# Adding an accumulator's two halves on ScalarE and GpSimd instead of TensorE

## The chip, the cores and the metric

One core of a Trainium2 chip runs the kernel. The metric is the device time of one execution in microseconds (us). The engines are TensorE (PE in the profile, its weight loads PEld), VectorE (DVE), ScalarE (ACT), GpSimd (POOL) and SyncE (SP), which here only starts DMA transfers. Each engine works through its own queue of instructions in the order in which the program wrote them, and a wait holds everything behind it on that engine.

## The reference

One layer of an encoder step for 288 tokens of width 2048: attention, a cross attention, a first norm, and then a mixture of 16384 single-neuron experts (128 x 128 product keys), of which each token chooses 128. The part that matters here is the experts' first product and its activation:

```python
def block(args):
    xs, es, gs = args
    act = jnp.einsum('td,tkd->tk', xs, u_tab[es], preferred_element_type=jnp.float32)
    h = (jax.nn.gelu(act, approximate=False) * gs).astype(xs.dtype)
    return jnp.einsum('tk,tkd->td', h, v_tab[es])
```

## The kernel before

The kernel treats 224 tokens densely: for them it computes the activations of all 16384 experts, in 128 blocks of 128 experts, sets the gates of the experts that were not chosen to zero, and multiplies with the value table. For the other 64 tokens it gathers the rows of the chosen experts with indirect DMAs on GpSimd (`fetch`, L944) and VectorE multiplies them (`use_u`, L963, into the gathered rows `ur`).

TensorE works on `float32r` operands of limited precision, so every large tensor is split into two parts: `hi` is a cast on ScalarE (L165), `lo` the remainder, raw minus hi, on VectorE (L181). The weights arrive as a stream of 128x1024 pieces, two per expert block ("half blocks"), through four raw buffers and three buffers each of `hi` and `lo`. `take` hands out the next piece and issues the cast of the piece two further on.

For one expert block (loop at L1031) an accumulator bank `ps` of 448 columns is filled by 16 pairs of products. The first of a pair multiplies `hi` with both parts of the tokens, `ux[:, d]`, side by side (448 columns, L1039). The second adds `lo` times the whole part (224 columns, L1041). So the left half of the bank holds the larger products and those of `lo`, and the right half the smaller ones, and both halves have to be added. `finish_act` (L989) does it, as a generator: it advances by one step at each `tick`, and there is a tick in the middle and at the end of every half block. Its first step comes right behind the block's last product: ScalarE copies the right half into `small`. At the next tick a product of `small` with the identity matrix adds it to the left half in the bank (L994). At the tick behind that ScalarE applies the Gelu from the bank into the block's row of the activations in SBUF, `hrow(i)` in the tensor `bigA` (L997).

`tick` also lets "slow" jobs proceed (mostly the choice of the experts, on VectorE, by a table of costs and a rate per tick), and then issues the `lo` that are due. From block 64 (`G0`) on the gates are built from one-hot matrices; until then `gated` is 0. The order of all engines' work is the order of this program text; nothing is rearranged later.

Of the kernel before, what the change touches and what calls it, by code (L numbers as in the profile page):

```python
# [9 lines left out]
F32 = mybir.dt.float32  # L10
# [4 lines left out]
OP = mybir.AluOpType  # L15
AX = mybir.AxisListType

P = 128
# [31 lines left out]
def tile_stream_step(ctx: ExitStack, tc, xT_d, xn_d, memT_d, ckT_d, cv_d, cmkT_d, cmv_d,  # L50
# [22 lines left out]
    def split_to(hi, lo, raw):  # L73
        """raw = hi + lo exactly, each part in the 12 bits that one pass of the tensor engine carries"""
        nc.scalar.copy(hi, raw)
        nc.vector.tensor_sub(lo, raw, hi.bitcast(F32))

    # x1 rows of the gathered tokens, and the expert choices
    keep = ctx.enter_context(tc.tile_pool(name="keep", bufs=1))
# [24 lines left out]

    # ------------------------------------------------ the stream of everything large
    def flat(t, a, b):
# [42 lines left out]
    def stream(n, ahead=AHEAD):  # L149
        """splits up to the weights that are ahead units after unit n, and loads beyond them"""  # L150
        until = n
        while until + 1 < len(plan) and ahead:
            until += 1
            ahead -= plan[until][2] is None
        while at["split"] <= until:
            k = at["split"]
            while at["load"] <= k:
                load_next()
            src, cols, hi, lo = plan[k]
            raw = loaded.pop(k)[:, :cols]  # L160
            if hi is None:
                hi, lo = own.get(k) or (strm.tile([P, 1024], F32R, tag=t, name=f"{t}{k}")[:, :cols] for t in ("hi", "lo"))
                parts[k] = (hi, lo)
            for cs in pieces(k):
                nc.scalar.copy(hi[:, cs], raw[:, cs])  # L165
                pending.append((k, hi[:, cs], lo[:, cs], raw[:, cs]))
                if k in PIECES:
                    settle()
            at["split"] += 1
        while at["load"] <= min(until + RAW - AHEAD, len(plan) - 1):  # L170
            load_next()
# [5 lines left out]
    def settle():  # L177
        """the small parts that are due"""
        while pending:
            _, hi, lo, raw = pending.pop(0)  # L180
            nc.vector.tensor_sub(lo, raw, hi.bitcast(F32))  # L181
# [23 lines left out]

    # ------------------------------------------------ work beside the stream
    stages = []          # each advances by one stage per tick
    slow = deque()       # one at a time, by its cost on the vector engine
    pace = {"rate": 0.0, "left": 0.0}
# [19 lines left out]
    def mm_tile(ps, part, k, d, mh, ml, n):  # L229
        """out^T [128 columns, n tokens] += one contraction tile of weights' (mh + ml)"""  # L230
        wh, wl = (w[:, k * P:(k + 1) * P] for w in part)
        nc.tensor.matmul(ps[:, :n], wh, mh[:, d, :n], start=(d == 0), stop=False)  # L232
        nc.tensor.matmul(ps[:, :n], wh, ml[:, d, :n], start=False, stop=False)  # L233
        nc.tensor.matmul(ps[:, :n], wl, mh[:, d, :n], start=False, stop=(d == DT - 1))  # L234

    def mm_unit(ps, half, mh, ml, n, ticks=(3, 7), tiles=8):
        """the next unit's contraction tiles"""
        part = take()
        for k in range(tiles):
            mm_tile(ps, part, k, half * 8 + k, mh, ml, n)  # L240
            for _ in range(ticks.count(k)):
                tick()

    def keep_warm(n):
        """products into a bank that nobody reads, so that the tensor engine's clock stays up over a pause"""
        ps = pb()
        for _ in range(n):
            nc.tensor.matmul(ps[:, :P], ident, ident, start=True, stop=True)
# [7 lines left out]
    def rsqrt(pool, out, v, n, rows=P):  # L256
        """out = (v + eps) ** -0.5, with a Newton step behind the square root's table"""
        t = pool.tile([P, 3, n], F32, tag=f"rs{n}", name=f"rs{num()}")[:rows]
# [7 lines left out]

    # ------------------------------------------------ constants, memory projections
    stream(-1, 1)
# [23 lines left out]
    def bias_job():  # L292
        """the relative bias of all heads, laid out by diagonals through DRAM"""
        for h in range(HEADS):
            ps = pb()
            nc.tensor.matmul(ps[:, :NREL], relb[:, h], hot, start=True, stop=True)
            yield
            nc.scalar.copy(bvec[:, h], ps[:, :NREL])
        nc.gpsimd.dma_start(bias_s, bvec.rearrange("p a b -> p (a b)"))
# [28 lines left out]

    # ------------------------------------------------ mixers
    ats = ExitStack()  # L330
# [44 lines left out]
    def diff_attend(h, qT, kT, vT, ck, cv):  # L375
# [51 lines left out]
        def weights(t):  # L427
            # w * s0 = e0 - lam * s0 / s1 * e1
            rows = TT[t][1]
# [153 lines left out]

    # ------------------------------------------------ output projection, first norm
    x1s = ExitStack()
# [26 lines left out]
    def residual(c, ps):  # L612
        """the tokens' rows again, added to the residual"""
        ot = nwk.tile([P, 3, P], F32, tag="ot", name=f"ot{c}", bufs=5)
# [46 lines left out]

    # ------------------------------------------------ expert choice
    ROWS = (P, 96, P)

    def topk(units):
        """the 16 best experts of heads for the tokens of their tiles: scores, and both halves of their numbers;
        the units' steps take turns"""
        V = nc.vector
# [88 lines left out]
    def dense_choice(t):  # L757
        """the choices of a dense token tile, its heads' units done"""
        yield from gates(t, 8)
# [25 lines left out]
    def rows_job():  # L785
        """x1 rows of the gathered tokens"""
        for a in range(2):
# [7 lines left out]
    def copy_job():  # L795
        """the dense tokens' part of x1, both parts side by side"""
        for d4 in range(4):
# [12 lines left out]
    def normed_turn(c):  # L810
        """a tile of the normed rows, transposed"""
        tp = pb()
# [100 lines left out]
    for q in range(2, 16):  # L913
        done(q, proj(x1h, x1l, NTOK))
    # the last scores, before the units of the experts
    while stages:
# [6 lines left out]

    # ------------------------------------------------ experts: activations and gates
    gat = ctx.enter_context(tc.tile_pool(name="gat", bufs=3))
# [5 lines left out]
    def hrow(i):  # L931
        return bigA[:, i] if i < SPLIT else big[1][2][:, i - SPLIT]
# [4 lines left out]
    class Rows:  # L937
        """half rows of the gathered tokens' experts, fetched ahead of their use"""

# [26 lines left out]
    def one_hots(t0):  # L966
        """of two tokens: the second key's choices, and the gates at the first key's"""
        Bt = big[2].tile([P, 2, NKEY], F32, tag="ohB", name=f"ohB{t0}")
# [9 lines left out]
    def gate_in(t0, ps, done):  # L978
        """gates of four tokens for all experts: into h where the activation is there, aside elsewhere"""
        pg = ps.rearrange("p (t i) -> p i t", t=4)  # L980
# [8 lines left out]
    def finish_act(i, ps, gated):  # L989
        """the smaller products onto the others, and the activation; h where the gates are there"""  # L990
        small = tmpp.tile([P, ND], F32R, tag="small", name=f"small{i}")
# [85 lines left out]

    # ------------------------------------------------ experts: values
    vw = ctx.enter_context(tc.tile_pool(name="vw", bufs=2, side="right"))
# [33 lines left out]
    def evac(half, dt, acc):  # L1113
        """the smaller products onto the others, and the sum onto the residual"""
        d = half * 8 + dt
# [21 lines left out]
    def finish_gathered():  # L1137
        """the gathered tokens' halves together, their second norm, out"""
        up = [gat.tile([P, 1024], F32, tag="rows", name=f"up{c}") for c in range(2)]
# [17 lines left out]
        for c in range(2):  # L1157
# [8 lines left out]
            if c == 0:  # L1166
# [3 lines left out]
                yield 4.0  # L1170
        # the rows of the dense tokens' norm, into what is free now
        for c in range(2):
# [12 lines left out]
    def turn(g, t):  # L1185
        """rows of a quarter of the columns again, in a free bank"""
        R = rows2[t]
# [8 lines left out]
    def products(half, dt, part, i):  # L1196
        """columns of the values (hi + lo) . a block's h, whole and remainder"""
        hb = batches[(half * NKEY + i) // 4][:, i % 4] if half or i else h0
# [7 lines left out]
    def finish(half, dt):  # L1206
        """a finished accumulator's evacuation, begun; the one before it, ended"""
        g = evac(half, dt, accs[dt])
# [65 lines left out]

    # ------------------------------------------------ second norm of the dense tokens
    fin = ctx.enter_context(tc.tile_pool(name="fin", bufs=1))
# [116 lines left out]
```

## Time and profile before

| | |
|---|---|
| runs | 2011.85, 2012.72, 2016.64 us; median 2012.72 |
| profiled execution | span 2008.1 us; a time of its own beside the span is not listed |
| busy in the whole span | PE 99%, PEld 93%, DVE 78%, ACT 58%, POOL 24% |
| expert blocks, first product | about 624 to 1336 us |
| of these the first 62 blocks | about 624 to 944 us |

The span goes from the first to the last instruction of one execution recorded by the profiler. Busy times of TensorE include the overlap of neighbouring products, so a single product's duration is longer than what it adds to the time. A name such as `lo<-raw,hi` is the tile that an instruction writes and those that it reads.

### The profile page before, as it was taken

To read this page: it belongs to the slowest core of one execution; us is meant where nothing else is said; L and a number is where in the kernel's file an instruction comes from. 1 tells how busy PE (TensorE), PEld (TensorE's weight loads), DVE (VectorE), ACT (ScalarE), POOL (GpSimd) and SP (SyncE) were. 2 spreads that over 40 slices of the span, in tenths; PEclk is the share of its full clock that TensorE was granted. 3 is DMA by queue.
4 is the path that set the end of the run, shared out by engine and by line. 5 is a ranking of instruction groups with operands and counts; after the bars stand their busy time and mean duration, and the time that the engine had idled before them with its cause. 6 is when DMAs were issued, how large, how long until landed. Compare 5 with 4: busy or idle time off the path is not lost.

```text
span 2008.1 us, 34989 instructions
## 1 busy us (share of the span) xinstructions
PE 1983.6 (99%) x13178; PEld 1872.5 (93%) x13178; DVE 1567.3 (78%) x2683; ACT 1160.7 (58%) x1919; POOL 480.9 (24%) x348
## 2 busy tenths in 40 slices
PE   9999999999999999999999999999999999999996
PEld 7999999999999999999999999999999999999996
DVE  5455555556788889998899999978888888888886
ACT  5345545544534555555999999854455555444553
POOL 0110000010000112222333333324443343334412
PEclk9999999999999999999999999999999999999998
DMA  8854555484445788888888888889999998999985
GB/s 294 258 165 141 153 155 153 129 287 137 154 148 162 241 291 280 277 282 283 294 298 296 293 298 302 300 288 318 335 322 343 327 333 314 323 328 321 327 264 167
DMA packets 147625, 521.21 MB, mean 260 GB/s; under 512 B 16848, under 2 KB 21088, under 8 KB 147328
## 3 DMA queue, kind: packets, MB, share of 16 engines
q1 hardware_dynamic: 103504, 360.49, 54.8%
q0 software_dynamic: 43952, 158.48, 22.0%
q8 instruction: 104, 1.70, 0.3%
q14 instruction: 65, 0.53, 0.1%
HBM read 508.33 MB, written 10.06 MB: 258 GB/s over the span
## 4 chain that ended last, share of the span: by engine, by line
PE 96%; DMA 1%; DVE 1%; ACT 1%; POOL 0%; issue 0%; SPq 0%; POOLq 0%; ACTq 0%; DVEq 0%
PE pa L1039 22%; PE pa L1200 11%; PE pb L1200 11%; PE pa L1041 11%; PE pa L232 8%; PE pa L233 7%; PE pa L234 7%; PE pb L1202 5%; PE pa L1202 5%; PE pb L1019 3%; DMA raw<-in_wmk 1%; PE pa L994 1%; PE pb L397 0%; DVE lo L181 0%; PE pa L893 0%; PE pa L319 0%
## 5 line engine op out<-in xcount | busy, mean ns | idle before, releaser
L181 DVE TENSOR_TENSOR lo<-raw,hi 128x1024 fp32r<-128x1024 f32 (+1 forms) x679 | 820.8, 1211 | 367.1 <-ACT hi L165 356.7
L165 ACT CAST hi<-raw 128x1024 fp32r<-128x1024 f32 (+1 forms) x679 | 705.5, 1040 | 497.2 <-PE pa L1200 253.8
L1039 PE MATMUL pa<-ux,hi 128*128 128x448 f32 x2048 | 669.8, 379 | 0.0
L1041 PE MATMUL pa<-ux,lo 128*128 128x224 f32 x2048 | 543.6, 265 | 0.0
L1039 PEld LDWEIGHTS pa<-ux,hi 128*128 128x128 f32 x2048 | 385.4, 188 | 29.4 <-issue 0.2
L1041 PEld LDWEIGHTS pa<-ux,lo 128*128 128x128 f32 x2048 | 391.7, 191 | 0.0
L948 POOL DMA_INDIRECT ur<-in_u,gidx x128 | 197.9, 1546 | 700.2 <-DVE ur L963 329.8
L1200 PE MATMUL pa<-hs,hi 128*128 128x448 f32 x1020 | 338.3, 376 | 0.0
L1200 PE MATMUL pb<-hs,hi 128*128 128x448 f32 x1020 | 338.0, 376 | 0.0
L948 POOL DMA_INDIRECT vr<-in_v,gidx x128 | 221.4, 1730 | 354.7 <-DVE x1g L1111 321.2
L1202 PE MATMUL pb<-hs,lo 128*128 128x224 f32 x1020 | 271.1, 266 | 0.3 <-DVE lo L181 0.3
L1202 PE MATMUL pa<-hs,lo 128*128 128x224 f32 x1020 | 271.0, 266 | 0.0
L1200 PEld LDWEIGHTS pb<-hs,hi 128*128 128x128 f32 x1020 | 191.4, 188 | 17.5
L1200 PEld LDWEIGHTS pa<-hs,hi 128*128 128x128 f32 x1020 | 191.4, 188 | 17.4
L1202 PEld LDWEIGHTS pb<-hs,lo 128*128 128x128 f32 x1020 | 195.1, 191 | 0.5 <-DVE lo L181 0.5
L232 PE MATMUL pa<-xh,hi 128*128 128x288 f32 x640 | 195.2, 305 | 0.0
L1202 PEld LDWEIGHTS pa<-hs,lo 128*128 128x128 f32 x1020 | 195.1, 191 | 0.0
L233 PE MATMUL pa<-xl,hi 128*128 128x288 f32 x640 | 188.9, 295 | 0.0
L234 PE MATMUL pa<-xh,lo 128*128 128x288 f32 x640 | 188.2, 294 | 0.0
L1111 DVE SCALAR_TENSOR_TENSOR x1g<-vr,ggate,x1g 128x1024 f32<-128x1024 f32 x128 | 163.7, 1279 | 0.0
L963 DVE SCALAR_TENSOR_TENSOR ur<-ur,x1g 128x1024 f32<-128x1024 f32 x128 | 155.7, 1216 | 0.0
L232 PEld LDWEIGHTS pa<-xh,hi 128*128 128x128 f32 x640 | 120.0, 188 | 4.9 <-issue 3.7
(346 smaller groups left out, 2706.7 us busy)
## 6 DMA issues: line engine op xcount, KB each, us to landing
raw<-in_ut SPq DMA_DIRECT2D x256, 512.0 KB, 4.4
raw<-in_v SPq DMA_DIRECT2D x255, 512.0 KB, 6.5
raw<-in_win SPq DMA_DIRECT2D x80, 512.0 KB, 3.7
raw<-in_wq SPq DMA_DIRECT2D x32, 512.0 KB, 3.6
raw<-in_wo SPq DMA_DIRECT2D x29, 512.0 KB, 3.7
raw<-in_wmv SPq DMA_DIRECT2D x8, 512.0 KB, 5.3
raw<-in_wmk SPq DMA_DIRECT2D x6, 512.0 KB, 5.8
xn<-in_xn POOLq DMA_DIRECT2D x8, 384.0 KB, 9.7
```

The costliest lines, as they stand in the source:

```text
L165: nc.scalar.copy(hi[:, cs], raw[:, cs])
L181: nc.vector.tensor_sub(lo, raw, hi.bitcast(F32))
L232: nc.tensor.matmul(ps[:, :n], wh, mh[:, d, :n], start=(d == 0), stop=False)
L233: nc.tensor.matmul(ps[:, :n], wh, ml[:, d, :n], start=False, stop=False)
L234: nc.tensor.matmul(ps[:, :n], wl, mh[:, d, :n], start=False, stop=(d == DT - 1))
L948: nc.gpsimd.indirect_dma_start(out=t, out_offset=None, in_=self.table, in_offset=bass.IndirectOffsetOnAxis(ap=gidx[:, a, s:s + 1], axis=0))
L963: nc.vector.scalar_tensor_tensor(rows, rows, 1.0, x1g[:, a * 1024:(a + 1) * 1024], op0=OP.mult, op1=OP.mult, accum_out=gact[:, a, s:s + 1])
L1039: nc.tensor.matmul(ps[:, :2 * ND], wh, ux[:, d].rearrange("p a t -> p (a t)"), start=(d == 0), stop=False, skip_group_check=True)
L1041: nc.tensor.matmul(ps[:, :ND], wl, ux[:, d, 0], start=False, stop=False, skip_group_check=True)
L1111: nc.vector.scalar_tensor_tensor(va, rows, ggate[:, s:s + 1], va, op0=OP.mult, op1=OP.add)
L1200: nc.tensor.matmul(accs[dt][:, :2 * ND], wh, hb.rearrange("p a t -> p (a t)"), start=(i == 0), stop=False, skip_group_check=True)
L1202: nc.tensor.matmul(accs[dt][:, :ND], wl, hb[:, 0], start=False, stop=False, skip_group_check=True)
```

## The change

For blocks 0 to 61 (`i < G0 - 2`) the accumulator's two halves are both copied to SBUF by ScalarE, the left half into the block's row of `bigA`, the right one into a tile `other`. At the next tick GpSimd adds the two, in place in `bigA`. Two ticks later ScalarE applies the Gelu, from `bigA` to `bigA`. Blocks 62 to 127 do as before. (Comments are dropped too, which moves line numbers: lines behind the new code are 10 higher.)

```diff
     def finish_act(i, ps, gated):
+        if i < G0 - 2:
+            other = tmpp.tile([P, ND], F32, tag="tmp", name=f"other{i}")
+            nc.scalar.copy(hrow(i), ps[:, :ND])
+            nc.scalar.copy(other, ps[:, ND:2 * ND])
+            yield
+            nc.gpsimd.tensor_tensor(out=hrow(i), in0=hrow(i), in1=other, op=OP.add)
+            yield
+            yield
+            nc.scalar.activation(hrow(i), hrow(i), AF.Gelu)
+            return
         small = tmpp.tile([P, ND], F32R, tag="small", name=f"small{i}")
         nc.scalar.copy(small, ps[:, ND:2 * ND])
         yield
         nc.tensor.matmul(ps[:, :ND], identr, small, start=False, stop=True, skip_group_check=True)
```

ScalarE's queue at the end of the first expert block, before (`hi` are the casts of the weights, `pa` the accumulator's bank):

```order
L165 CAST hi_6879<-raw_6767 128x1024
L992 CAST small_6901<-pa_6846 128x224
L165 CAST hi_6904<-raw_6850 128x1024
L997 ACT_TABLE_LOAD
L997 ACTIVATE bigA<-pa_6846 128x224
L165 CAST hi_6938<-raw_6882 128x1024
L992 CAST small_6960<-pa_6903 128x224
```

The same place in the changed kernel:

```order
L165 CAST hi_6879<-raw_6767 128x1024
L993 COPY bigA<-pa_6846 128x224
L994 COPY other_6901<-pa_6846 128x224
L165 CAST hi_6905<-raw_6850 128x1024
L165 CAST hi_6938<-raw_6882 128x1024
L999 ACT_TABLE_LOAD
L999 ACTIVATE bigA<-bigA 128x224
L993 COPY bigA<-pa_6904 128x224
```

There are two copies where there was one, and the Gelu stands behind the second cast instead of the first.

GpSimd's queue where the gathers of rows (`ur`) begin, before:

```order
L948 DMA ur_1_7617<-in_u,gidx 128x1024
L948 DMA ur_0_7701<-in_u,gidx 128x1024
L948 DMA ur_1_7763<-in_u,gidx 128x1024
L948 DMA ur_0_7852<-in_u,gidx 128x1024
L948 DMA ur_1_7930<-in_u,gidx 128x1024
```

And in the changed kernel:

```order
L948 DMA ur_1_7628<-in_u,gidx 128x1024
L996 TENSOR_TENSOR bigA<-bigA,other_7657 128x224
L948 DMA ur_0_7714<-in_u,gidx 128x1024
L996 TENSOR_TENSOR bigA<-bigA,other_7716 128x224
L948 DMA ur_1_7777<-in_u,gidx 128x1024
L996 TENSOR_TENSOR bigA<-bigA,other_7779 128x224
L996 TENSOR_TENSOR bigA<-bigA,other_7831 128x224
L948 DMA ur_0_7867<-in_u,gidx 128x1024
```

The adds are put between the gathers, one per expert block; TensorE's queue is 62 products shorter, and VectorE's is the same.

## Rows read from the trace of the kernel before

**Rows 1.** The page: busy us of the whole span, share, instructions.
```profile
PE 1983.6 (99%) x13178; PEld 1872.5 (93%) x13178; DVE 1567.3 (78%) x2683; ACT 1160.7 (58%) x1919; POOL 480.9 (24%) x348
```
**Rows 2.** Waits of TensorE, 624 to 965 us: total us, times, longest.
```profile
PE pb L832 <- ACT qT L860: 0.5, 1, 0.5
```
**Rows 3.** Busy us by stretch: PE, PEld, DVE, ACT, POOL; clock, DMA share, GB/s.
```profile
684.00:724.00 40.00, 40.00 (x259) 38.00 (x258) 37.90 (x98) 21.25 (x31) 12.10 (x8) 1.00 0.88 303
...
774.00:794.00 20.00, 20.00 (x130) 19.00 (x129) 19.27 (x45) 10.81 (x16) 4.29 (x3) 1.00 0.86 284
...
814.00:864.00 50.00, 50.00 (x322) 47.51 (x321) 47.27 (x115) 26.21 (x40) 12.68 (x8) 1.00 0.83 276
...
874.00:934.00 60.00, 60.00 (x385) 57.02 (x384) 55.81 (x124) 31.12 (x47) 11.38 (x9) 1.00 0.86 281
...
sum 340.00, PE 340.00 PEld 322.95 DVE 301.47 ACT 191.25 POOL 62.40; mean PE 37.78 PEld 35.88 DVE 33.50 ACT 21.25 POOL 6.93
```
**Rows 4.** Timeline of TensorE around one L994: start us, duration us.
```profile
801.44 0.27 PE L1041 MATMUL pa<-ux,lo 128*128 128x224 f32 x1
801.54 0.27 PE L994 MATMUL pa<-small,identr 128*128 128x224 f32 x1
801.65 0.37 PE L1039 MATMUL pa<-ux,hi 128*128 128x448 f32 x1
```
**Rows 5.** The same without L994, at the border of two half blocks.
```profile
722.48 0.26 PE L1041 MATMUL pa<-ux,lo 128*128 128x224 f32 x1
722.59 0.38 PE L1039 MATMUL pa<-ux,hi 128*128 128x448 f32 x1
722.80 0.27 PE L1041 MATMUL pa<-ux,lo 128*128 128x224 f32 x1
```
**Rows 6.** The chain of waits, 620 to 970 us, shares by line.
```profile
by line: PE pa L1039 64.6%; PE pa L1041 31.4%; PE pa L994 2.0%; PE pb L1019 0.5%; PE pa L232 0.4%; PE pa L234 0.3%; PE pa L233 0.3%; PE pb L763 0.2%; PE pb L832 0.1%; ACT qT L860 0.1%; PE pb L834 0.1%; PE pb L833 0.1%; issue 0.0%
```
**Rows 7.** Line 994 from 620 to 970 us: durations ns min/median/max.
```profile
L994 PE MATMUL pa<-small,identr x66: 269/273/275, 631.0 to 968.3; 128*128 128x224 f32 x66
```
**Rows 8.** Timeline of ScalarE from 800 us.
```profile
800.48 0.35 ACT L992 CAST small<-pa 128x224 fp32r<-128x224 f32 x1 [1.58 <-PE pa L1041]
800.72 1.05 ACT L165 CAST hi<-raw 128x1024 fp32r<-128x1024 f32 x1
...
803.01 1.05 ACT L165 CAST hi<-raw 128x1024 fp32r<-128x1024 f32 x1 [0.80 <-PE pa L1039]
805.63 0.34 ACT L992 CAST small<-pa 128x224 fp32r<-128x224 f32 x1 [1.57 <-PE pa L1041]
```
**Rows 9.** Timeline of VectorE at 802 us.
```profile
802.53 1.20 DVE L181 TENSOR_TENSOR lo<-raw,hi 128x1024 fp32r<-128x1024 f32 x1
```
**Rows 10.** Timeline of GpSimd at the end of the kernel.
```profile
1997.31 1.26 POOL L1295 TENSOR_TENSOR fo<-fo,bb 128x512 f32<-128x512 f32 x1
...
1998.53 1.71 POOL L1295 TENSOR_TENSOR fo<-fo,bb 128x512 f32<-128x512 f32 x1
```
**Rows 11.** Timeline of VectorE from 718 us.
```profile
718.54 1.22 DVE L963 SCALAR_TENSOR_TENSOR ur<-ur,x1g 128x1024 f32<-128x1024 f32 x1
...
721.09 2.35 DVE L181 TENSOR_TENSOR lo<-raw,hi 128x1024 fp32r<-128x1024 f32 x2
```
**Rows 12.** Timeline of GpSimd at 720 us.
```profile
720.04 0.93 POOL L948 DMA_INDIRECT ur<-in_u,gidx  x1 [5.63 <-DVE ur L963]
```
**Rows 13.** Timeline of ScalarE from 720 us.
```profile
720.16 1.05 ACT L165 CAST hi<-raw 128x1024 fp32r<-128x1024 f32 x1 [0.80 <-PE pa L1039]
```
**Rows 14.** Timeline of VectorE at the end of the kernel, beside rows 10.
```profile
1997.13 0.74 DVE L1287 SCALAR_TENSOR_TENSOR fo<-pa,mr,x1g 128x512 f32<-128x512 f32 x1
1997.90 1.22 DVE L1297 SCALAR_TENSOR_TENSOR fo<-fo,mr,bb 128x512 f32<-128x512 f32 x1
```
**Rows 15.** Costliest groups of VectorE, 624 to 965 us: busy us, mean ns.
```profile
L181 DVE TENSOR_TENSOR lo<-raw,hi 128x1024 fp32r<-128x1024 f32 x131 | 159.5, 1221 | 37.5 <-ACT hi L165 35.1 <-PE pa L1041 1.6
...
L963 DVE SCALAR_TENSOR_TENSOR ur<-ur,x1g 128x1024 f32<-128x1024 f32 x42 | 51.0, 1213 | 0.0
```

## Prediction

> **What bounds the kernel now.** I read the busy shares first, then the same shares in the stage that the change touches, then the waits of TensorE there, then single instructions. The page gives TensorE 99% of the span [rows 1]; in the stage it is busy without a gap, at a granted clock of 1.00, the 2.4 GHz level [rows 3]. A busy share alone proves little, so I looked at who waits: from 624 to 965 us, 65 expert blocks with all of the change in them, TensorE waited once, 0.5 us, for a copy at the very start [rows 2]. So the stage lasts as long as TensorE's products take one after the other, and a product that is taken out shortens it directly, as long as nobody else becomes late. The one that could become late is VectorE: it is busy 301.5 of 340 us there [rows 3], and TensorE needs its `lo` tile before each half block. ScalarE is busy 191 of 340 us and GpSimd 62 of 340 [rows 3]; both have room.
>
> **What is removed: 62 products with the identity.** A row's own duration (0.27 us) is no price, since products overlap; the price is the distance between starts. With the product, the last L1041 starts at 801.44, L994 at 801.54, the next L1039 at 801.65: 0.21 us from L1041 to L1039 [rows 4]. Without one, L1041 starts at 722.48 and L1039 at 722.59: 0.11 us [rows 5]. The difference is 0.10 us. The chain of waits says the same over many: L994 is 2.0% of the 350 us from 620 to 970, 7.0 us [rows 6], for 66 products [rows 7], so 0.106 us each. **Term 1: 62 x 0.106 = 6.6 us less.** Both the weight load and the later reading of the sum by the Gelu were hidden, so there is no more to win here.
>
> **ScalarE.** Per block one copy of 224 columns becomes two. One took 0.35 us, and the next instruction starts 0.24 us behind it (800.48 to 800.72 [rows 8]). So 62 x 0.24 to 0.35 = 15 to 22 us more work go into 340 - 191 = 149 us of idle time [rows 3]. What matters is the cast `hi` that is queued behind the copies: it starts 0.24 us later, at about 800.96 instead of 800.72, in every first half of a block. Its `lo` ended at 803.73 [rows 9] for the half block that begins when `small` is next copied, at 805.63 [rows 8]: 1.9 us early. 0.24 us fits. Nothing on the path.
>
> The Gelu is moved behind the next `hi` and reads the sum from SBUF; I cost its new source at nothing, since it lies in that idle time. It now waits for GpSimd, and behind it stand the next block's copies and then a `hi`. At 800 us the second copy would end near 801.1 and the Gelu's turn comes when the `hi` that started at 803.01 ends, at 804.06 [rows 8]: the add has 3.0 us.
>
> **GpSimd.** 62 adds of 128x224 are new. The nearest rows are the five adds of 512 columns at the end of the kernel: 1.26 us for the undisturbed one [rows 10]. Below, in proportion to the columns, 1.26 x 224/512 = 0.55 us; above, all of it being fixed cost, 1.26 us. I take 0.6 us, near the proportional end, as every instruction shown has some fixed part. That is 34 to 78 us in 340 - 62 = 278 us of idle time. The Trainium skill (GPSIMD Engine Reference, section 3.1) states 4497 ns for such an add of 2048 columns; the line through it and the 1.26 us would give 0.66 us, called an estimate. With it the term of VectorE below would grow by a tenth.
>
> The queue matters more. The adds stand between the gathers (L948), and a gather waits until VectorE has used up the buffer (L963). Near 718 us such a use ends at 719.76 [rows 11], the gather's descriptors run from 720.04 to 720.97 [rows 12], and only then the add. With 0.6 us it ends at 721.6, with 1.26 us at 722.2. ScalarE's turn for the Gelu comes at 721.21 [rows 13], and that for the next copies when the block's last product ends, at 722.74 [rows 5]. So ScalarE would stand for half a microsecond in its own idle time. Nothing on the path, with half a microsecond left at the long end.
>
> **VectorE and GpSimd together.** This is the cost that the trace of before hardly shows, because GpSimd computes nothing beside VectorE in that stage. It does at the end. An L1297 instruction of 128x512, which reads two tiles from SBUF, took 1.22 us while GpSimd was adding; L1287 of the same size, with one input from PSUM, took 0.74 [rows 14]. GpSimd's add at that time took 1.71 us instead of 1.26 [rows 10]. Each lost 0.45 to 0.48 us to the other: they take turns. In the stage, the two kinds of VectorE work with two SBUF inputs are L181 and L963, 159.5 + 51.0 = 210.5 us of 341 [rows 15], 62% of the time. So most adds meet one. What VectorE loses per add lies between 0 (the add falls into idle time or beside one-input work, or waits itself) and 1.26 us. I take 0.3 us: half of a 0.6 us add, since in somewhat less than half of the meetings the next instruction of VectorE needs no second SBUF input, or the add does the waiting.
>
> Then VectorE's work grows by 62 x 0.3 = 19 us against 38.5 us of idle time, while TensorE leaves 6.6 us less. On the whole it fits. But the idle time is not spread evenly. Four stretches are packed: 684 to 724, 774 to 794, 814 to 864, 874 to 934 us, together 170 us with 37.9 + 19.3 + 47.3 + 55.8 = 160.3 us busy [rows 3], 9.7 us idle. At 5.15 us a block (two copies of `small`, 800.48 and 805.63 [rows 8]) these are 33 blocks: 33 x 0.3 = 9.9 us more work in 33 x 0.106 = 3.5 us less time. VectorE would be 3.7 us over, 0.9 us in each stretch. Against this stands the time by which `lo` is early: 1.9 us at 803.73, as shown, and at the tightest place I found, the two `lo` from 721.09 to 723.44, of which the first ends half way, at 722.26 [rows 11], 0.54 us before the first product that reads it, at 722.80 [rows 5]. So 0.9 us is covered at most places and comes through by some tenths at a few. **Term 2: 0.8 us of new waits** (0 at the lower end; the upper end is the second and third rival).
>
> **The sum.** -6.6 + 0.8 = -5.8 us, from a span of 2008.1 to 2002.3 us. The median of the runs, 2012.7, lies 4.6 us above that span; I carry this over: **2006.9 us**, 0.29% less. A measurement of this kernel can tell about 0.3%, 6.0 us, from no change; the forecast sits right at that line. All behind the stage keeps its pace, since TensorE sets it there as well [rows 1], and the transfers have slack: their share is 0.83 to 0.88 in these stretches [rows 3].
>
> **Rivals.**
> (a) *Full gain.* All adds fall into idle time: -6.6 us, 2006.1. For it: 38.5 us of idle time and 3.0 us for each add. I count it with the forecast, as both lie within 2005.6 to 2007.7 us: together 0.60.
> (b) *VectorE gives part of it back.* It loses 0.4 to 0.5 us per add. In the four stretches, 33 x 0.5 = 16.5 us more work and 3.5 us less time against 9.7 us idle: 10.3 us over. Of this an early `lo` covers in each stretch some 1.2 us (the middle between 0.54 and 1.9), 4.8 in all, so 5.5 us come through: 2011.6. With 0.4 us per add it is 7.0 - 4.8 = 2.2 us, and 2008.3. For it: a use of gathered rows and two `lo`, with two-input work between them, fill 718.5 to 723.4 us [rows 11], so there an add always meets two-input work. Chance 0.28.
> (c) *VectorE becomes the bound: slower.* The place is the same packed stretches, the price the whole hold of an add. It decides from about 0.7 us lost per add: 23.1 us more work (33 x 0.7), + 3.5 - 9.7 = 16.9 over, less 4.8, is 12.1 us of waits against the 6.6 us gain: 2018.2. At 1 us per add it would be 22.0 us of waits and 2028.1. For it: with two-input work on both sides, VectorE stands for the add's full length. Against: the add then has to last near what 512 columns took. The Trainium skill (SBUF — State Buffer, section Who interferes with whom) states that such a VectorE instruction and a GpSimd one that reads SBUF exclude each other for the whole instruction, and speaks against this change. The rows above agree that they take turns; no row of this trace shows an add amid such a queue. Chance 0.12, of which 0.10 end over 0.3% slower.
> (d) *The change doesn't do it.* Excluded by the order: TensorE's queue is 62 products shorter. A late add that holds ScalarE, and with it `hi`, would need more than the 3.0 us and the cushion of `lo`; it is in (c).
>
> **Range and chances.** The range runs from 2005.2, the full gain with the runs' small scatter, to 2012.5, the end of (b): about 0.85 of the cases. Faster by over 0.3% means below 2006.7: two thirds of the forecast with (a), 0.40. Slower by over 0.3%: 0.10 of (c). The rest, 0.50, is within.
>
> **What would show it.** Right: TensorE's line of waits stays near empty in the stage; the distance L1041 to L1039 is 0.11 us everywhere in the first 62 blocks; the stage is 5.8 us shorter; adds of about 0.6 us; L181 somewhat over 1.22 us in the mean, with VectorE's busy time up by about 19 us. Wrong: waits of TensorE for `lo` (L181) of several microseconds in the packed stretches would be (b) or (c); waits for `hi` (L165) behind a Gelu that waits for GpSimd would be the queue; adds of over 1 us would sink the sum.

## Result and profile after

The changed kernel takes 2025.17 us in the median (2024.69 to 2028.54), against 2013.74 us before: a ratio of 1.0061, 95% interval 1.0046 to 1.0076. It is slower by 0.6%, where I had forecast 0.3% less, and lies above the range (2005.2 to 2012.5 us). The profiled execution took 2024.77 us, its span is 2023.0 us, 14.9 us above that of before.

Where the time went is seen in the waits of the first expert blocks. These are the waits of the changed kernel from 600 to 1000 us (who waited on which line, for whom: total us, times, longest):

```profile
ACT bigA L999 <- POOL bigA L996: 73.9, 28, 6.6
...
PEld pa L1051 <- DVE lo L181: 16.8, 20, 5.2
```

TensorE, which had waited once for 0.5 us [rows 2], now waits for `lo` 20 times. ScalarE waits 28 times, 74 us, at the Gelu (L999) for GpSimd's add (L996). Neither row has a counterpart before.

The four packed stretches again, in the same columns as [rows 3]:

```profile
684.00:724.00 40.00, 34.83 (x208) 32.51 (x207) 31.68 (x83) 18.96 (x34) 16.23 (x13) 0.91 0.74 252
774.00:794.00 20.00, 19.54 (x121) 17.85 (x120) 16.80 (x38) 10.99 (x20) 11.12 (x6) 1.00 0.77 253
814.00:864.00 50.00, 48.90 (x308) 45.81 (x308) 46.09 (x111) 26.24 (x46) 25.18 (x17) 1.00 0.83 275
874.00:934.00 60.00, 57.96 (x360) 53.52 (x359) 54.64 (x130) 33.70 (x59) 32.27 (x21) 1.00 0.81 266
```

TensorE is no longer busy throughout, and VectorE is not busier: 149.2 us in these 170, where it was 160.3 [rows 3]. So it is not that VectorE has no time left. GpSimd's busy time there has doubled. The first stretch has lost most.

The costliest groups from 624 to 965 us (busy us, mean ns, then idle time before them):

```profile
L181 DVE TENSOR_TENSOR lo<-raw,hi 128x1024 fp32r<-128x1024 f32 x126 | 154.7, 1238 | 30.2 <-ACT hi L165 30.0
...
L996 POOL TENSOR_TENSOR bigA<-bigA,other 128x224 f32<-128x224 f32 x62 | 90.6, 1462 | 268.8 <-DMA raw<-in_ut 209.3 <-ACT other L994 58.7
...
L963 DVE SCALAR_TENSOR_TENSOR ur<-ur,x1g 128x1024 f32<-128x1024 f32 x39 | 47.9, 1229 | 6.3 <-DMA ur<-in_u,gidx 6.3
```

VectorE's two kinds of two-input work are hardly longer than before (1238 and 1229 ns against 1221 and 1213 [rows 15]). The add is: 1.46 us in the mean. Line 996 by itself (min/median/max in ns):

```profile
L996 POOL TENSOR_TENSOR bigA<-bigA,other x62: 660/828/4928, 630.9 to 959.5; 128x224 f32<-128x224 f32 x62
```

The shortest add takes 0.66 us, 26 of the 62 take under 0.70, the longest 4.93.

**One long add and what hangs on it.** Three engines from 865 to 875 us, GpSimd first:

```profile
866.75 1.69 POOL L948 DMA_INDIRECT ur<-in_u,gidx  x1 [3.64 <-DVE ur L963]
868.47 4.80 POOL L996 TENSOR_TENSOR bigA<-bigA,other 128x224 f32<-128x224 f32 x1
```

VectorE at the same time:

```profile
868.59 0.74 DVE L699 TENSOR_TENSOR ca<-sv 96x256 f32<-96x256 f32 x2
869.25 1.22 DVE L181 TENSOR_TENSOR lo<-raw,hi 128x1024 fp32r<-128x1024 f32 x1
870.39 1.22 DVE L963 SCALAR_TENSOR_TENSOR ur<-ur,x1g 128x1024 f32<-128x1024 f32 x1
871.53 0.08 DVE L963 DVE_READ_ACCUMULATOR ur<-ur,x1g 128x1 f32 x1
871.53 1.22 DVE L181 TENSOR_TENSOR lo<-raw,hi 128x1024 fp32r<-128x1024 f32 x1
872.67 0.72 DVE L703 CAST sf<-si 96x32 f32<-96x32 uint32 x2
```

And ScalarE:

```profile
867.73 1.05 ACT L165 CAST hi<-raw 128x1024 fp32r<-128x1024 f32 x1 [1.58 <-DMA raw<-in_ut]
873.30 0.39 ACT L999 ACTIVATE bigA<-bigA 128x224 f32<-128x224 f32 x1 [4.52 <-POOL bigA L996]
873.60 0.33 ACT L993 COPY bigA<-pa 128x224 f32<-128x224 f32 x1
```

TensorE behind that:

```profile
875.46 0.37 PE L1049 MATMUL pa<-ux,hi 128*128 128x448 f32 x1
876.44 0.37 PE L1051 MATMUL pa<-ux,lo 128*128 128x224 f32 x1 [0.61 <-DVE lo L181]
```

The add first stands behind a gather, which waited 3.64 us until VectorE had used up a buffer. It begins at 868.47, and VectorE runs two-input work without a gap from 868.59 to 872.75. The add ends at 873.27, about 0.5 us behind that: it got nothing done while the chain lasted. It is not the only one: of the 25 adds that took over 1 us, 17 end 0.51 to 0.55 us behind the end of a VectorE instruction with two SBUF inputs. ScalarE stands 4.52 us for the add at the Gelu, the next block's copies and casts come late, and TensorE's product of 876.44 waits 0.61 us for `lo`. How many of the smaller waits come about like this, one trace does not tell; the run with the later Gelu below does.

**The large wait.** GpSimd and then VectorE around the first use of gathered rows; for comparison, the first gather of the kernel before started at 685.72 and its rows were used at 690.94 without a wait:

```profile
685.97 0.73 POOL L996 TENSOR_TENSOR bigA<-bigA,other 128x224 f32<-128x224 f32 x1 [3.66 <-ACT other L994]
686.87 1.02 POOL L948 DMA_INDIRECT ur<-in_u,gidx  x1 [0.17 <-DVE si L684]
```
```profile
695.51 1.23 DVE L963 SCALAR_TENSOR_TENSOR ur<-ur,x1g 128x1024 f32<-128x1024 f32 x1 [6.33 <-DMA ur<-in_u,gidx]
696.66 0.08 DVE L963 DVE_READ_ACCUMULATOR ur<-ur,x1g 128x1 f32 x1
696.66 1.22 DVE L181 TENSOR_TENSOR lo<-raw,hi 128x1024 fp32r<-128x1024 f32 x1
```

The row numbers were ready (L781) at 682.6. But an add stood ahead of the gather, and it waited for ScalarE's copies until 685.97. So the gather began at 686.87, VectorE reached its use at 689.2, stood 6.33 us for the transfer, and the `lo` behind it came late. The later start is only half of it. Before, the gather began 0.96 us after the row numbers were ready, and its rows landed 5.2 us later, just in time; here it began 4.25 us after them, and the rows took 8.6 us to land. The runs below with as late a first gather show long landings too (7.3 us with the late Gelu, 7.7 us with later gathers), those with a prompt one 5.7 to 6.1 us. Why a late gather also lands slowly, no run separates. TensorE:

```profile
692.61 0.38 PE L1049 MATMUL pa<-ux,hi 128*128 128x448 f32 x1
697.93 0.56 PE L1051 MATMUL pa<-ux,lo 128*128 128x224 f32 x1 [4.94 <-DVE lo L181]
```

5.3 us lie between two starts that are 0.21 us apart elsewhere. The product behind the wait takes 0.56 us instead of 0.27, the next ones of its line 0.39. The granted clock from 697.7 to 702.0 us was 0.52 of full speed, about the lower of the two levels (1.2 GHz):

```profile
697.70:702.00 4.30, 4.07 (x14) 3.81 (x15) 4.30 (x17) 0.39 (x1) 2.64 (x2) 0.52 0.65 223
```

That is another 4.3 x 0.48 = 2 us. From the first product of the stage to the last, the changed kernel took 13.1 us more (624.8 to 1349.2 against 624.6 to 1335.9 us, start to start). With the 6.6 us that the removed products should have given, some 20 us were lost: 5.1 and 2 us here, most of the rest in the 19 smaller waits for `lo`, 11.6 us together.

### The profile page after: what moved, and what is told of

Same layout as the page of the kernel before. It is cut to its first block, busy times and chain, and to the rows that moved or that the text cites. A ratio compares the mean times of both kernels' runs of the same rounds, so it can differ in the third digit from the quotient of the medians.

```text
span 2023.0 us, 34984 instructions
## 1 busy us (share of the span) xinstructions
PE 1984.3 (98%) x13116; PEld 1866.6 (92%) x13116; DVE 1577.6 (78%) x2683; ACT 1170.9 (58%) x1981; POOL 575.9 (28%) x410
## 4 chain that ended last, share of the span: by engine, by line
PE 91%; DVE 4%; POOL 1%; DMA 1%; ACT 1%; issue 1%; SPq 0%; POOLq 0%; DVEq 0%; ACTq 0%
PE pa L1049 18%; PE pa L1210 11%; PE pb L1210 11%; PE pa L1051 9%; PE pa L232 8%; PE pa L233 7%; PE pa L234 7%; PE pb L1212 5%; PE pa L1212 5%; PE pb L1029 3%; DVE lo L181 1%; POOL bigA L996 1%; DVE ur L963 1%; DMA raw<-in_wmv 1%; ACT hi L165 1%
## 5 line engine op out<-in xcount | busy, mean ns | idle before, releaser
L1049 PE MATMUL pa<-ux,hi 128*128 128x448 f32 x2048 | 668.7, 379 | 0.0
L1051 PE MATMUL pa<-ux,lo 128*128 128x224 f32 x2048 | 547.1, 267 | 11.5 <-DVE lo L181 11.3
L1049 PEld LDWEIGHTS pa<-ux,hi 128*128 128x128 f32 x2048 | 386.1, 189 | 30.0 <-issue 0.2
L1051 PEld LDWEIGHTS pa<-ux,lo 128*128 128x128 f32 x2048 | 392.2, 192 | 17.4 <-DVE lo L181 16.8
L996 POOL TENSOR_TENSOR bigA<-bigA,other 128x224 f32<-128x224 f32 x62 | 90.6, 1462 | 268.8 <-DMA raw<-in_ut 209.3
## 6 DMA issues: line engine op xcount, KB each, us to landing
xn<-in_xn POOLq DMA_DIRECT2D x8, 384.0 KB, 10.3
```

The source lines that it names most:

```text
L1049: nc.tensor.matmul(ps[:, :2 * ND], wh, ux[:, d].rearrange("p a t -> p (a t)"), start=(d == 0), stop=False, skip_group_check=True)
L1051: nc.tensor.matmul(ps[:, :ND], wl, ux[:, d, 0], start=False, stop=False, skip_group_check=True)
```

## Experiments

I held two theories from here. **Held Gelu:** a late add stops ScalarE at the Gelu, `hi` and then `lo` are late; this is the larger part. **First gather:** an add that waits for ScalarE stands ahead of the first gather; this is the single large wait. The rival was what I had reckoned with before: the adds slow VectorE itself. All ratios are against the kernel before on the same chip. Differences in microseconds between two variants are differences of medians, some of them from two chips.

**No add.** Takes the `gpsimd.tensor_tensor` out of the changed kernel.

> The changed kernel without the adds on GpSimd: the smaller products of the first 62 blocks are left out. Theory (the adds hold up others, the removed products are worth 6.6 us): ratio to the kernel before 0.9967 (2007 us), no wait of TensorE for lo in the stage, and VectorE does not wait for the first gathered rows. Rival (ScalarE's second copy, or the products are worth less): 0.999 to 1.001.

2005.13 us, ratio 0.9961 (0.9947 to 0.9976), span 2002.1. No wait for `lo` in the stage, none of VectorE for gathered rows. Term 1 is confirmed: 6.0 us by the spans, 5 to 11 by the interval. If the two copies on ScalarE cost anything, it is too little to show.

**Gelu one block later.**

```diff
             nc.gpsimd.tensor_tensor(out=hrow(i), in0=hrow(i), in1=other, op=OP.add)
-            yield
-            yield
+            for _ in range(6):
+                yield
             nc.scalar.activation(hrow(i), hrow(i), AF.Gelu)
```

> The changed kernel with the Gelu four ticks (one block) later, so that ScalarE need not wait for a late add. Theory (about 12 us of the loss come by ScalarE standing at the Gelu, so that hi and then lo are late; 8 us come from the first gather and stay): ScalarE's 74 us of waits for L996 fall to under 5 us, ratio 0.999 to 1.001 (2013 us). Rival (the adds slow VectorE itself, and lo is late for that): waits of TensorE stay near 20 us, ratio 1.004 to 1.006.

2014.16 us, ratio 1.0011 (1.0002 to 1.0020): 11 us less than the changed kernel. The Gelu has no wait left, and TensorE's waits for `lo`, from 600 to 1400 us, are few:

```profile
PEld pa L1051 <- DVE lo L181: 5.9, 4, 3.8
```

Beside the longest, 3 waits with 2.1 us are left of 19 with 11.6 us. The adds are not shorter (1.54 us in the mean), and VectorE's busy time over the span is no smaller (1580.9 us against 1577.6 in the changed kernel). So for the larger part it was not the adds' length by itself that cost the time, nor VectorE's loss, but ScalarE standing behind them. The ratio ends just above the 0.999 to 1.001 that I gave. The longest wait, 3.8 us, is the one at the first gather; VectorE still stands 5.0 us there.

**First gathers earlier.** The three first gathers are issued as soon as their row numbers are there, two half blocks before the first use.

```diff
                 if g_from is None:
                     g_from = n
+                    for k in range(3):
+                        ug.fetch(k)
```

> The changed kernel with the first three gathers issued two half blocks earlier, ahead of the add that stood before them. Theory (that add's wait for ScalarE's copies delays the first gather, VectorE stands 6.3 us at its first use and TensorE loses 5.1 us plus 2.9 us at half clock): the wait near 692 us is gone, 8 us less, ratio 1.002 (2017 us). Rival (the wait near 692 us has another cause, the transfers are simply slow there): ratio stays at 1.006.

2022.17 us, ratio 1.0044 (1.0029 to 1.0058). VectorE's wait for the rows is gone, as the theory said, but the gain is 3.0 us by the medians (3.6 by the spans), not 8, and the interval overlaps that of the changed kernel, so the time alone does not show a gain. The other waits stayed (ScalarE stands 75.3 us for adds here): those of TensorE for `lo` come to 13.2 us, where all but the large one had come to 11.6. Part of what the large wait had cost came back in them.

**Both.**

> Both edits together, Gelu one block later and the first gathers earlier. Theory: nearly the full gain of the 62 products, 6 us, ratio 0.997 (2007 us). Rival (VectorE loses time to the adds): 1.000 to 1.003.

2010.27 us, ratio 0.9984 (0.9974 to 0.9994). Both edits together win 14.9 us, about the sum of 11.0 and 3.0, and the kernel is faster than before. The intervals of this run and of the late Gelu alone do not overlap, so here the earlier gathers do gain. About half of the full gain is still missing, and the ratio lies between those of the theory and of the rival. TensorE has 4.0 us of waits for `lo` left; VectorE's busy time (1579.9 us) is as high as in the other runs with adds on GpSimd. What the remaining waits come from, no run separates.

**Gathers after the next half block.** To tell apart why the adds are late, this one issues each further gather one half block after the use that frees its buffer. Fewer adds should then stand behind a waiting gather; the order of VectorE's work is unchanged.

```diff
-                self.fetch(g + 3)
+                self.due.append(g + 3)
```
with `upto` issuing what is `due` before anything else.

> The changed kernel with each further gather issued one half block after the use that frees its buffer, so that an add seldom stands behind a gather that waits for VectorE. The first gathers are as in the changed kernel. Theory (the adds are late for two reasons, the gather ahead of them in the queue and VectorE's chains; this takes the first away): ScalarE's waits for the adds fall from 74 to 35 to 60 us, ratio 1.001 to 1.004, with the 5 us wait near 692 us still there. Rival (only VectorE's chains matter): waits and ratio as in the changed kernel, 1.006.

2016.26 us, ratio 1.0012 (0.9999 to 1.0024), 8.9 us less. The gathers waited 24 times for VectorE to free a buffer, where it had been 33 times (both from 624 to 985 us). ScalarE's wait in this run, from 624 to 985 us:

```profile
ACT bigA L1004 <- POOL bigA L1001: 26.3, 12, 5.7
```

From 73.9 us to 26.3, more than expected, while the adds are as long as ever (1.51 us in the mean, 5.79 at most). So about two thirds of the time that ScalarE stands come from the place in GpSimd's queue, behind a gather that waits for VectorE; where adds start in time, their starving uses up the 3 us they have in 12 of 62 blocks at most. The wait at the first gather is there too (4.3 us of TensorE), as it should.

**A write-only instruction in place of the add.** `nc.gpsimd.memset(other, 0.0)`.

> The changed kernel with a memset of 128x224 on GpSimd in place of each add (the smaller products of the first 62 blocks are left out; GpSimd reads nothing from SBUF, and the Gelu does not wait for it). Theory (GpSimd's reads are what VectorE's two-input chains keep out): every memset takes the same time, below 0.6 us, none over 1 us. Rival (any GpSimd work on SBUF is kept out): durations up to several us as those of the adds. Ratio for both near 0.997 to 1.001, as the memset still waits for ScalarE's copy in the gathers' queue.

2010.28 us, ratio 0.9993 (0.9983 to 1.0003). Line 996 in this run:

```profile
L996 POOL MEMSET other<- x62: 279/299/304, 630.9 to 942.9; 128x224 f32 x62
```

All 62 take the same time, also the 26 that lie wholly beside VectorE's work with two SBUF inputs. What VectorE's chains keep out is GpSimd's reading. And though it lasts 0.3 us and holds no Gelu, VectorE stood 4.6 us for the first gathered rows:

```profile
693.82 1.23 DVE L963 SCALAR_TENSOR_TENSOR ur<-ur,x1g 128x1024 f32<-128x1024 f32 x1 [4.59 <-DMA ur<-in_u,gidx]
```

The first gather is late because of the wait ahead of it, not because an add is long.

**Openings in VectorE's chain.** A one-column memset on VectorE behind each `lo`, and in a second run, instead of it, a search for the eight largest of 128 columns (the diff shows both lines):

```diff
             nc.vector.tensor_sub(lo, raw, hi.bitcast(F32))
+            if mark:
+                nc.vector.memset(mark[0], 0.0)
+                nc.vector.max(out=mark[0], in_=iota)
```

> The changed kernel, with a one-column memset on VectorE behind every lo from the first gather to block 61, about 100 in all. Theory (an add that meets a chain of VectorE instructions with two SBUF inputs stands until the chain ends; any instruction without a second SBUF input between them lets it in): the longest adds fall from 4.9 us to about 2.5 us, the mean from 1.46 to about 1.1 us, ScalarE's waits for L996 fall from 74 to some 40 us. Ratio 1.002 to 1.005, as VectorE also loses time to adds that now get in. Rival (the adds are slow for another reason, such as the gathers' descriptors): durations as before, mean 1.4 to 1.5 us, longest near 4.9.

> As e6, with a search for the eight largest of 128 columns (one SBUF input, 0.28 us in the trace) in place of the one-column memset behind each lo. Theory (an opening in VectorE's two-input chain lets an add in if it is long enough; the 0.06 us of the memset was not): longest add below 3 us, mean about 1.2 us; ScalarE's waits for L996's add below 60 us, while VectorE has 100 x 0.2 = 20 us more work, so the time is 1.004 to 1.010 of that before. Rival (single one-input instructions do not open the chain): mean 1.4 us or more and longest add over 4 us.

The first: 2025.5 us, ratio 1.0063 (1.0048 to 1.0077). The second has a single execution, 2027.5 us, too few for a ratio with an interval. The add in the one and in the other:

```profile
L1000 POOL TENSOR_TENSOR bigA<-bigA,other x62: 664/826/4947, 636.8 to 965.0; 128x224 f32<-128x224 f32 x62
```
```profile
L1000 POOL TENSOR_TENSOR bigA<-bigA,other x62: 662/688/4971, 631.1 to 964.5; 128x224 f32<-128x224 f32 x62
```

Here I missed. The memset of 0.06 us changes next to nothing (mean 1.41 us against 1.46). The search of 0.28 us shortens the mean to 1.23 us, but the longest add is as long as before, and ScalarE still stands 70.0 us for adds (68.2 with the memset). The longest add of that run stood through two of the searches, which are L184 here:

```profile
806.59 4.97 POOL L1000 TENSOR_TENSOR bigA<-bigA,other 128x224 f32<-128x224 f32 x1
```
```profile
808.30 0.28 DVE L184 MAX8 gap<-iota 128x8 f32<-128x128 f32 x1
808.50 1.20 DVE L182 TENSOR_TENSOR lo<-raw,hi 128x1024 fp32r<-128x1024 f32 x1
809.62 0.28 DVE L184 MAX8 gap<-iota 128x8 f32<-128x128 f32 x1
```

So not any instruction without a second SBUF input lets an add in, and 0.28 us is not always enough. What decides it stays open.

**All three.** Late Gelu, early first gathers and the memsets.

> Late Gelu, early first gathers, and the one-column memsets together. Theory: the adds are shorter than in e4 (mean 1.76 us there) and the gathers behind them earlier, so that little is left but VectorE's own loss: ratio 0.997 to 0.999. Rival (what is left in e4 is VectorE's lost time, which the memsets raise): 0.999 to 1.002.

2007.54 us, ratio 0.9973 (0.9962 to 0.9984). That meets the number, but after the run above not for the stated reason: the adds are hardly shorter than with the two edits alone (1.62 us in the mean against 1.76). The interval overlaps that of the two edits alone, so I don't call it a gain of the memsets.

**The add on VectorE.** VectorE adds the bank's left half and ScalarE's copy of the right one; only one copy is needed, and GpSimd does nothing.

```diff
-            nc.scalar.copy(hrow(i), ps[:, :ND])
             nc.scalar.copy(other, ps[:, ND:2 * ND])
             yield
-            nc.gpsimd.tensor_tensor(out=hrow(i), in0=hrow(i), in1=other, op=OP.add)
+            nc.vector.tensor_tensor(out=hrow(i), in0=ps[:, :ND], in1=other, op=OP.add)
```

> The changed kernel with the add on VectorE, which reads the left half from the accumulator's bank and the right half from ScalarE's copy; GpSimd adds nothing, and ScalarE copies one half, not two. Theory (the loss came from GpSimd's adds, which starve beside VectorE's work and stand in the queue of the gathers; VectorE has room for about 0.37 us per block, 23 us in all): ratio 0.997 to 0.999 (2008 us), no wait of ScalarE for GpSimd. Rival (VectorE's packed stretches are the limit, whoever adds): TensorE waits for lo by 6 us or more, ratio 1.000 to 1.003.

2006.28 us, ratio 0.9969 (0.9958 to 0.9981); on another chip 2006.92 us and 0.9968 (0.9955 to 0.9981):

> The kernel of e5 again, to stand beside e9 on the same chip: ratio 0.996 to 0.998, as before.

The add, from 624 to 975 us:

```profile
L995 DVE TENSOR_TENSOR bigA<-pa,other 128x224 f32<-128x224 f32 x62 | 23.7, 382 | 2.5 <-ACT other L993 2.4
```

The engine that I had thought too full spends 24 us on the adds and holds hardly anyone: ScalarE's Gelu waits 1.9 us in all, TensorE 1.6 us for `lo`. This version beats both kernels.

**The same in all 128 blocks.** The product with the identity goes in blocks 62 to 127 as well.

> The add on VectorE in all 128 blocks: in blocks 62 to 127 too it adds the bank's left half and ScalarE's copy, into the copy, from which the Gelu reads. Theory (66 more products go, 7.0 us, but VectorE is over 90% busy there and the Gelu now waits for it): the gain of e5 grows only in part, ratio 0.995 to 0.998. Rival (VectorE becomes the bound behind block 62): TensorE waits for lo by over 7 us there, ratio 0.998 to 1.005.

2030.46 us, ratio 1.0083 (1.0064 to 1.0101). Slower, but not as the rival had it: TensorE waits for `lo` for 0.7 us only. From 964 to 1345 us, ScalarE first, then TensorE:

```profile
ACT tmp L1010 <- DVE small L1003: 45.0, 43, 2.2
```
```profile
PEld pb L1029 <- ACT ohA L975: 29.5, 73, 0.5
```

ScalarE stands 45 us at the Gelu for VectorE's sum, and TensorE then waits for the one-hot matrices that ScalarE makes behind it (and 7.3 us for those that VectorE makes). Before, with the sum from TensorE, the Gelu waited 12.7 us there, 0.2 us at most each time. By these rows it is the held Gelu once more, with another engine holding it; no run tests that apart.

## Why the prediction was wrong

**Term 1 was right.** Six to seven microseconds for the 62 products: the kernel without adds shows 6.0 by the spans. The distance from L1051 to L1049 is 0.11 us where nothing waits (801.48 to 801.59).

**The undisturbed add was right.** I took 0.6 us; it is 0.66. The line through the Trainium skill's figure (GPSIMD Engine Reference, section 3.1) and the 1.26 us gives an estimate of 0.65, where the prediction has 0.66; the trace agrees with it.

**The step that failed is "Nothing on the path", in the part on GpSimd.** With the part on ScalarE it gave the add 0.55 to 1.26 us, 3.0 us of room, and half a microsecond left at the place that I looked at. The add took 4.93 us at the longest, 1.46 us in the mean. My sum had put the whole price of the contention on VectorE and nothing on the add. The rows at the end of the kernel showed each side losing 0.45 to 0.48 us, one instruction against one; I carried that "they take turns" into a stage where VectorE runs four or five such instructions in a row. There the add waits for all of them. The prediction even had the place: rival (b) says that two-input work fills 718.5 to 723.4 us, and in those very microseconds the part on GpSimd lets the add end at 721.6 or 722.2. Standing through that chain it would have ended near 723.9 (an estimate: the chain's end and the 0.5 us that an add takes behind one), over 1 us after ScalarE's turn for the next copies. (The changed kernel's work had shifted against that chain, and its add of 720.27 took 0.85 us; the add of 868.47 shows the same case.) And the 3.0 us were counted for an add that starts at once, while the one behind a waiting gather starts late. The run with later gathers took away two thirds of ScalarE's waits. ScalarE stood 73.9 us at the Gelu, which the sum had at nothing, and the run with the later Gelu gives 11 us of the time back. I had seen the queue, worked out one instance of it, and taken that for the worst.

**A wait was missing: the first gather behind an add.** I asked what the adds wait for behind the gathers, not what the gathers wait for behind the adds. The first three gathers are the only ones whose rows are needed at once. The wait there cost 5.1 us plus some 2 us at the lower clock; about half of VectorE's wait is the late start, the other half a slower transfer whose cause is open.

**Term 2, VectorE's loss, was too high in its price, and its sum of waits came about in another way.** I took 0.3 us per add; VectorE's busy time over the whole span rose by 10.3 us (1567.3 to 1577.6), 0.17 us per add. TensorE's waits for `lo` came to 16.8 us instead of 0.8, and most of them went when the Gelu came later, with VectorE as busy as before.

**Rival (c) had the sign, not the mechanism.** It wanted VectorE as the bound, with 0.7 us or more lost per add; that 2025 us lies between its two figures is luck. The late add that holds ScalarE stood under (d) and was set aside with one sentence, without a price of its own. The Trainium skill (SBUF — State Buffer, section Who interferes with whom) says that a VectorE instruction with two SBUF inputs contends with a GpSimd instruction that reads SBUF, not with one that only writes it, and that the port pair that the two share is an exclusive lock. The rows agree that an add gets nothing done meanwhile, and that a GpSimd instruction that only writes is free. They also show an add that came first, and the `lo` beside it took 1.38 us instead of 1.22:

```profile
748.90 0.68 POOL L996 TENSOR_TENSOR bigA<-bigA,other 128x224 f32<-128x224 f32 x1
749.28 1.38 DVE L181 TENSOR_TENSOR lo<-raw,hi 128x1024 fp32r<-128x1024 f32 x1 [1.24 <-ACT hi L165]
```

And they add that the loser can stand through a whole chain: the add of 868.47 stood through five instructions, one after the other. It had begun 0.12 us before the first of them, but as it ended 0.52 us behind the last, 0.14 us short of an undisturbed add's 0.66, the rows do not tell which of the two reached for SBUF first.

## What to carry to other kernels

An in-order engine that takes over a small step also takes over its queue: ask for each neighbour in that queue, in both directions, what it waits for, and who stands behind the result. Work that reads SBUF on GpSimd beside a VectorE that runs two-input instructions back to back should have no one waiting for it within the length of the longest such chain. A nearly full engine that keeps its order may be the better place for the step than an idle one with a queue of waits: VectorE, at 89% in this stage, took the adds of the 62 blocks and, as far as the times can tell, kept the whole gain. In the other 66 blocks, where ScalarE makes other things behind the Gelu, the same step lost time, so the place has to be checked stage by stage.

## What I had not expected of the hardware

GpSimd's add of 128x224 took 0.66 us alone and up to 4.93 us beside VectorE, which itself was slowed by about 1% (1238 against 1221 ns for `lo`). A memset of the same size took 0.28 to 0.30 us in all 62 instances. An instruction of 0.06 us without SBUF inputs between VectorE's two-input ones hardly let the add in (1.41 us in the mean against 1.46), and one of 0.28 us did so only in part (1.23 us). After TensorE had stood for 5 us, its granted clock was 0.52 of full speed for the first 4.3 us of work.
